# A gMLP layer and a sliding-window attention layer on one core: k's low part at full height over zeros, and both sets of PSUM banks for q, k with v, and z

## The chip, the core and the metric

The kernel runs on one core of one Trainium2 chip. The metric is the device time of one execution in microseconds (us); three runs of the kernel before gave a median of 1056.93 us (1056.63 to 1057.12). Profiles are taken of one execution, with a row for each instruction of each engine: PE (TensorE, matrix products; its weight loads are listed as PEld), DVE (VectorE), ACT (ScalarE), POOL (GpSimd) and SP (SyncE, which here only issues DMAs).

## The reference

1024 tokens of width 1024, float32. One gMLP layer, then one attention layer with 16 query heads over 4 shared key/value heads of width 64, a window of 128, attention sinks and ALiBi. Cut to what matters:

```python
u, v, z = split(rms_norm(h) @ w_in, 3)                 # gMLP, width 2048
v = layer_norm(gelu(v))
s = einsum('gts,bnsgc->bntgc', tril(w_s), v) + b_s     # inside chunks of 128 tokens
h = h + rms_norm((gelu(u) * s * silu(z)) @ w_out)
kv_in = rms_norm(h)
k, v = kv_in @ w_k, kv_in @ w_v                        # 4 heads of 64
q, z = split(rms_norm(h) @ b_w_in, 2)
logits = (q / 8) @ k.T + alibi                         # block of 128 queries, 256 keys
p = exp(logits - m); o = (p @ v) / (sum(p) + exp(sink - m))
h = h + rms_norm((o * silu(z)) @ b_w_out)
```

## The kernel before

Nearly every product is made from operands in the fp32r form, split into a high part and a low part (hi = rounded, lo = rest), as three products hi*hi, hi*lo and lo*hi that accumulate in one PSUM bank (`mm3`, lines 168 to 171). ACT makes the high part and DVE the low part, of weights (`split`, `split_scaled`, lines 104 to 110) as of activations. PSUM has two sets of four banks of 128 x 512: tag "mm" and tag "s" (`bank`, line 81).

The stages stand one behind another: the v layer (to about 150 us), u and z with the spatial mixing (to about 500 us), the first output layer, and from about 653 us the attention layer, in two halves of 512 tokens, h = 0 and h = 1. In its order, lines 1197 to 1226:

1. `q_phase(0)`: q of half 0 in two groups of four row blocks of 128 (`qz_four`), each group 4 weight pieces x 24 products into four "mm" banks (tiles qz). ACT and DVE move each bank out in two steps each (lines 969 and 970): q_hi holds the high part of q for the even head's 64 rows and the low part in the other 64 rows, q_lo the other way round. Beside it runs `chain_a(1)`, the residual sum of half 1, and the first steps of `norm_h1(1)`.
2. `kv_phase(0)`: k and v of half 0 (tiles pk, pv; lines 987 to 1013), in four "mm" banks. The high part of k goes into all 128 rows of kh[par] (the same 64 rows twice), its low part into 64 rows of one tile kl.
3. `z_phase(0)`: z of half 0, two groups in "mm" banks, and between its products the rest of `norm_h1(1)`: 8 groups of four transposes (tiles nt, line 769) into "s" banks, which ACT and DVE split into n1.
4. `attn(0)`: units of one block of 128 queries and one pair of key heads. `scores` (lines 1022 to 1065) makes, twice per unit, two banks of scores with 8 products: four of full height (128 rows: q's high and low part against the doubled kh, lines 1040 to 1044), then four of half height (64 rows: q's high part against kl, lines 1045 to 1050). The softmax follows on DVE and ACT, `transposes` (tiles pt) on PE, the causal masks on POOL (tiles pc, pp), `values` (tile o, products 64 columns wide), and the gate and the split on DVE and ACT. Between those steps `fill` hands out products of k, v, q and z of half 1.
5. `attn(1)`, with the last z and the output layer of half 0 (`out_b0`) as its fill; then `out_b1`.

Inside a program each engine runs its instructions in a fixed order. That order comes from a scheduler which may move independent instructions past each other, so it is not the text's. The weights go through two buffers of whi and wlo: piece n+2 can be split once the products of piece n are done.

In the v layer (`v_layer`, lines 291 to 505) the products come in steps (Q, m, u); after a step ACT moves banks out, and the lines 492 to 496 (`late`) apply the gelu to four tiles of a past sum and store them.

Of the kernel before, what the change touches and what calls it, by code (L numbers as in the profile page):

```python
# [50 lines left out]
def tile_yoco(  # L51
# [239 lines left out]
    def v_layer(ahead):  # L291
# [141 lines left out]
        for n, (Q, m, u) in enumerate(steps):  # L433
# [19 lines left out]
            if n == 0:  # L453
                xload(xa[:, 1], 0, 1, 0, 2)
            elif n == 1:
                prep(3)
                xload(xa[:, 1], 0, 1, 2, 2)
            elif n >= 4:
                step(side)
            if u == 0:  # L460
                continue
# [29 lines left out]

            late = {6: (a1, 0), 4: (e67, 1)}.get(m) if Q == 0 else None
            if late:
                for t in range(4):
                    done(late[0][t], late[0][t], late[1], late[1], t, Q)
                store(slots[late[1]], late[1], late[1], Q)
# [263 lines left out]
    def norm_h1(h, n, yo):  # L760
        for t in range(4):
# [180 lines left out]
    kl = bp.tile([P, 2, S], F32R, name="kl")  # L942
# [8 lines left out]
    def qz_four(h, which, m, n, evac):  # L951

        ps = [bank("mm", f"qz{h}_{which}_{m + i}") for i in range(4)]
# [33 lines left out]
    def kv_phase(h, n):  # L987
# [18 lines left out]
        hs = slice(h * TH, (h + 1) * TH)  # L1006
        for i in range(2):
            for par in range(2):
# [3 lines left out]
                nc.vector.tensor_tensor(kl[rw, i, hs], pk[i][rw], kh[par][rw, i, hs].bitcast(F32), ALU.subtract)  # L1012
            nc.vector.tensor_copy(vt[:, h * 4 + 2 * i:h * 4 + 2 * i + 2].rearrange("p a b -> p (a b)"), pv[i])

    class Unit:
# [6 lines left out]
        def scores(self, gp):  # L1022
# [16 lines left out]

            for g in range(2):  # L1040
                m = p * 4 + gp * 2 + g
                for par in range(2):
                    nc.tensor.matmul(pss[par][:, g, w0:256], lhsT=q[par][:, m, bs_], rhs=kh[par][:, p, ks],
                                     start=g == 0, stop=False, skip_group_check=True)
            for g in range(2):
                m = p * 4 + gp * 2 + g
                for par in range(2):
                    rw = half[par]
                    nc.tensor.matmul(pss[par][:, g, w0:256], lhsT=q[par][rw, m, bs_], rhs=kl[rw, p, ks],
                                     start=False, stop=g == 1, skip_group_check=True)  # L1050
# [80 lines left out]
    def out_b0(y, yo, gp):  # L1131
        ss = const.tile([P, 2, 4], F32, tag="ss", name="ssb0")
        for gd in range(2):
            ps = [bank("mm", f"ob0_{gd}_{t}") for t in range(4)]
            for cp in range(4):
                hi, lo = wnext()
                for j in range(2):
# [7 lines left out]
                    yield  # L1145
            for t in range(4):
                evac_out(yo[t], ss, ps[t], t, gd, gp, "ob0")
# [10 lines left out]
    def final(h, t, yo, ss, r=None):  # L1158
        r = final_rstd(h, t, ss) if r is None else r
        xt = load_tok(h1d[h][t], f"hf{h}_{t}")  # L1160
        for i in range(2):
            cs = slice(i * 512, i * 512 + 512)
            nc.vector.scalar_tensor_tensor(yo[:, cs], yo[:, cs], r, xt[:, cs], ALU.mult, ALU.add)
            if (h, t) == (1, 3) or i == 1:
                cs = cs if (h, t) == (1, 3) else slice(0, D)
                (nc.scalar if (h, t, i) == (1, 3, 1) else nc.sync).dma_start(
# [121 lines left out]
```

## Time and profile before

| | |
|---|---|
| median of 3 runs | 1056.93 us |
| the profiled execution, its own time | 1056.3 us |
| its span, first to last instruction | 1054.4 us |
| mean granted TensorE clock | 0.999 |
| busy: PE, DVE, ACT, POOL | 1042.8, 731.9, 577.0, 194.7 us |

Read it so: a row of the timeline has the start and the length of an instruction in us, its engine, its line, its output and inputs, their shapes, and how often it follows itself; behind it, in brackets, the idle time of the engine before it and whose end ended that. Products overlap in the array, so the length of one is not what it costs. What it costs is the distance from its start to the start of the next one: two of 128 x 512 start 0.227 us apart in undisturbed stretches.

### The profile page before, as it was taken

To read this page: it belongs to the slowest core of one execution; us is meant where nothing else is said; L and a number is where in the kernel's file an instruction comes from. 1 tells how busy PE (TensorE), PEld (TensorE's weight loads), DVE (VectorE), ACT (ScalarE), POOL (GpSimd) and SP (SyncE) were. 2 spreads that over 40 slices of the span, in tenths; PEclk is the share of its full clock that TensorE was granted. 3 is DMA by queue.
4 is the path that set the end of the run, shared out by engine and by line. 5 is a ranking of instruction groups with operands and counts; after the bars stand their busy time and mean duration, and the time that the engine had idled before them with its cause. 6 is when DMAs were issued, how large, how long until landed. Compare 5 with 4: busy or idle time off the path is not lost.

```text
span 1054.4 us, 13649 instructions
## 1 busy us (share of the span) xinstructions
PE 1042.8 (99%) x4994; PEld 849.3 (81%) x4994; DVE 731.9 (69%) x1244; ACT 577.0 (55%) x989; POOL 194.7 (18%) x151
## 2 busy tenths in 40 slices
PE   9999999999999999999999999999999999999997
PEld 7788788888888888888888888788887777777776
DVE  7987467867767768678696587745257876667763
ACT  6684443555565555555444474645466665686631
POOL 0500003254343542540200000000000111011120
PEclk9999999999999999999999999999999999999999
DMA  8877352334333434338997542632222121221363
GB/s 319 270 274 265 100 180 83 122 110 138 119 116 115 150 106 134 111 131 279 328 337 273 190 149 93 210 100 91 94 75 72 40 81 61 80 61 60 121 218 120
DMA packets 79890, 157.55 MB, mean 149 GB/s; under 512 B 5712, under 2 KB 32592, under 8 KB 79824
## 3 DMA queue, kind: packets, MB, share of 16 engines
q1 hardware_dynamic: 75168, 147.75, 41.2%
q10 hardware_dynamic: 4656, 8.94, 2.4%
q8 instruction: 39, 0.64, 0.2%
q14 instruction: 27, 0.22, 0.1%
HBM read 125.21 MB, written 31.46 MB: 149 GB/s over the span
## 4 chain that ended last, share of the span: by engine, by line
PE 92%; DVE 4%; issue 2%; DMA 1%; ACT 0%; POOL 0%; DVEq 0%; POOLq 0%; ACTq 0%
PE ob L169 6%; PE ub L169 6%; PE ub L171 6%; PE ob L170 6%; PE ub L170 6%; PE ob L171 6%; PE qz L169 5%; PE qz L170 5%; PE qz L171 5%; PE uc L170 3%; PE uc L169 3%; PE uc L171 3%; PE sp L614 3%; PE vb L169 2%; PE vb L170 2%; PE vb L171 2%
## 5 line engine op out<-in xcount | busy, mean ns | idle before, releaser
L169 PE MATMUL qz<-n_hi,whi 128*128 128x512 f32 x256 | 102.8, 402 | 2.2 <-DVE q_lo L970 2.1
L110 DVE SCALAR_TENSOR_TENSOR wlo<-raw_w,gn,whi 128x512 fp32r<-128x512 f32 x80 | 58.3, 758 | 63.9 <-ACT whi L109 63.6
L170 PE MATMUL qz<-n_lo,whi 128*128 128x512 f32 x256 | 100.0, 391 | 0.0
L171 PE MATMUL qz<-n_hi,wlo 128*128 128x512 f32 x256 | 99.9, 390 | 0.0
L109 ACT ACTIVATE whi<-raw_w,gn 128x512 fp32r<-128x512 f32 x80 | 54.6, 716 | 55.6 <-PE qz L170 25.8
L1064 ACT ACTIVATE pr<-pr,mx 128x129 f32<-128x129 f32 x128 | 50.0, 393 | 42.1 <-DVE mx L1060 41.8
L169 PEld LDWEIGHTS qz<-n_hi,whi 128*128 128x128 f32 x256 | 48.0, 188 | 21.3 <-issue 9.2
L105 ACT ACTIVATE uzhilo_g<-f 128x1024 fp32r<-128x1024 f32 x31 | 32.9, 1060 | 49.7 <-PE uc L171 43.8
L171 PEld LDWEIGHTS qz<-n_hi,wlo 128*128 128x128 f32 x256 | 48.1, 188 | 10.5
L170 PEld LDWEIGHTS qz<-n_lo,whi 128*128 128x128 f32 x256 | 48.1, 188 | 9.0
L106 DVE TENSOR_TENSOR uzhilo_g<-f,uzhilo_g 128x1024 fp32r<-128x1024 f32 x31 | 38.6, 1246 | 20.1 <-ACT uzhilo_g L105 20.1
L209 ACT ACTIVATE uz_slots<-ub 128x512 f32<-128x512 f32 x48 | 28.3, 589 | 42.1 <-PE ub L171 38.9
L169 PE MATMUL ub<-T,whi_g 128*128 128x512 f32 x128 | 50.7, 396 | 0.0
L169 PE MATMUL ub<-T,uzhilo_g 128*128 128x512 f32 x128 | 50.5, 395 | 0.0
L171 PE MATMUL ub<-T,wlo_g 128*128 128x512 f32 x128 | 49.9, 390 | 0.0
L171 PE MATMUL ub<-T,uzhilo_g 128*128 128x512 f32 x128 | 49.9, 390 | 0.0
L170 PE MATMUL ub<-T,uzhilo_g 128*128 128x512 f32 x128 | 49.8, 389 | 0.0
L170 PE MATMUL ub<-T,whi_g 128*128 128x512 f32 x128 | 49.8, 389 | 0.0
L169 PE MATMUL uc<-T,uzhilo_g 128*128 128x512 f32 x124 | 48.9, 395 | 0.0
L170 PE MATMUL uc<-T,uzhilo_g 128*128 128x512 f32 x124 | 48.3, 389 | 0.0
L171 PE MATMUL uc<-T,uzhilo_g 128*128 128x512 f32 x124 | 48.3, 389 | 0.0
L105 ACT ACTIVATE whi_g<-raw_uz 128x1024 fp32r<-128x1024 f32 (+1 forms) x31 | 26.5, 854 | 36.9 <-PE ua L170 14.6
(326 smaller groups left out, 3058.9 us busy)
## 6 DMA issues: line engine op xcount, KB each, us to landing
raw_uz<-in_wuz_in_dram SPq DMA_DIRECT2D x32, 512.0 KB, 3.4
raw_w<-in_wqz_dram SPq DMA_DIRECT2D x32, 512.0 KB, 3.5
td<-uz_slots SPq DMA_DIRECT2D x56, 256.0 KB, 2.1
orawP2a<-td SPq DMA_DIRECT2D x28, 512.0 KB, 4.0
raw<-in_wv_in_dram SPq DMA_DIRECT2D x17, 512.0 KB, 4.7
vg<-vd SPq DMA_DIRECT2D x8, 1024.0 KB, 5.3
orawP2b<-in_wo_a_dram SPq DMA_DIRECT2D x16, 512.0 KB, 8.0
vraw<-in_wv_in_dram SPq DMA_DIRECT2D x13, 512.0 KB, 4.8
```

The costliest lines, as they stand in the source:

```text
L105: nc.scalar.activation(hi, src, AF.Copy)
L106: nc.vector.tensor_tensor(lo, src, hi.bitcast(F32), ALU.subtract)
L109: nc.scalar.activation(hi, src, AF.Copy, scale=g)
L110: nc.vector.scalar_tensor_tensor(lo, src, g, hi.bitcast(F32), ALU.mult, ALU.subtract)
L169: nc.tensor.matmul(out, lhsT=a_hi, rhs=b_hi, start=start, stop=False, skip_group_check=True)
L170: nc.tensor.matmul(out, lhsT=a_hi, rhs=b_lo, start=False, stop=False, skip_group_check=True)
L171: nc.tensor.matmul(out, lhsT=a_lo, rhs=b_hi, start=False, stop=stop, skip_group_check=True)
L209: nc.scalar.activation(out, a, AF.Copy)
L614: nc.tensor.matmul(psv[:, n], lhsT=d["vg"][:, 4 * j + n, i * P:(i + 1) * P], rhs=d["wc"], start=True, stop=True)
L1064: nc.scalar.activation(pr[:, i], pr[:, i], AF.Exp, bias=mx[:, i:i + 1], scale=-1.0, accum_out=dn[:, i:i + 1])
```

## The change

Four edits that belong together, and two that follow from them.

- The low part of k gets two tiles, kl[0] and kl[1], each 128 rows high, with k's low part in the head's own 64 rows and zeros in the other 64, which POOL writes once (`memset`). The low product of a score now reads all 128 rows of q[par]. The loop puts the low product of a bank right behind its high product.
- kl[1] lies in the buffer P1_3, which held two token blocks of `yo` of half 1. So `norm_h1(1)` takes the blocks in the order 2, 3, 0, 1, and runs between the products of `kv_phase(0)`, not of `z_phase(0)`.
- The second group of q and the first group of z of half 0 go into "s" banks.
- P1_3 is taken until the end of attention, so the output of half 0 is kept in two halves: columns 0 to 511 in P1_0, columns 512 to 1023 in the weight buffers whi and wlo. Each token block of the final output is stored with two DMAs of 512 columns, not one of 1024.
- In the v layer the four late gelus with their store stand one step (24 products) later.

```diff
--- before.py
+++ after.py
@@ -457,6 +457,12 @@
                 xload(xa[:, 1], 0, 1, 2, 2)
             elif n >= 4:
                 step(side)
+
+            late = {(7, 0): (a1, 0), (3, 0): (e67, 1)}.get((m, u)) if Q == 0 else None
+            if late:
+                for t in range(4):
+                    done(late[0][t], late[0][t], late[1], late[1], t, Q)
+                store(slots[late[1]], late[1], late[1], Q)
             if u == 0:
                 continue
             for t in range(4):
@@ -488,12 +494,6 @@
                 block = (slots[0], 0, 0) if m == 2 else (slots[1], 1, 1)
             if block:
                 store(*block, Q)
-
-            late = {6: (a1, 0), 4: (e67, 1)}.get(m) if Q == 0 else None
-            if late:
-                for t in range(4):
-                    done(late[0][t], late[0][t], late[1], late[1], t, Q)
-                store(slots[late[1]], late[1], late[1], Q)
             if m == 3:
                 a1, e67 = [], []
             if Q == 1 and m == 2:
@@ -757,8 +757,8 @@
         rstd(r1[h], s1, f"h1{h}")
         yield
 
-    def norm_h1(h, n, yo):
-        for t in range(4):
+    def norm_h1(h, n, yo, order=range(4)):
+        for t in order:
             xt = st.tile([P, D], F32, tag="xt", name=f"hb{h}_{t}")
             nc.vector.tensor_scalar(xt, yo[t], r1[h][:, t:t + 1], None, ALU.mult)
             yield
@@ -939,7 +939,8 @@
     nc.vector.memset(neg, -1e30)
 
     kh = [bp.tile([P, 2, S], F32R, name=f"kh{i}") for i in range(2)]
-    kl = bp.tile([P, 2, S], F32R, name="kl")
+
+    kl = [bp.tile([P, 2, S], F32R, name="kl0")]
     qsc = bp.tile([P, 2], F32, name="qsc")
     nc.sync.dma_start(out=qsc, in_=consts[:, C_QS:C_QS + 2])
     snk = bp.tile([P, 4, 4], F32, name="snk")
@@ -950,7 +951,8 @@
 
     def qz_four(h, which, m, n, evac):
 
-        ps = [bank("mm", f"qz{h}_{which}_{m + i}") for i in range(4)]
+        tag = "s" if (h, which, m) in ((0, 0, 4), (0, 1, 0)) else "mm"
+        ps = [bank(tag, f"qz{h}_{which}_{m + i}") for i in range(4)]
         for kq in range(4):
             hi, lo = (t.rearrange("p (m k c) -> p m k c", m=4, k=2) for t in wnext())
             for i in range(4):
@@ -1004,12 +1006,17 @@
                         hi[:, vs], lo[:, vs], k == 0 and t4 % 2 == 0, k == KT - 1 and t4 % 2 == 1)
                 yield
         hs = slice(h * TH, (h + 1) * TH)
+        if h == 0:
+            kl.append(big.tile([P, 2, S], F32R, tag="P1_3", name="kl1"))
+            for par in range(2):
+                zero = kl[par][half[1 - par]].bitcast(F32)
+                nc.gpsimd.memset(zero.rearrange("p a b -> p (a b)"), 0.0)
         for i in range(2):
             for par in range(2):
                 rw, ot = half[par], half[1 - par]
                 nc.scalar.activation(kh[par][rw, i, hs], pk[i][rw], AF.Copy)
                 nc.scalar.activation(kh[par][ot, i, hs], pk[i][rw], AF.Copy)
-                nc.vector.tensor_tensor(kl[rw, i, hs], pk[i][rw], kh[par][rw, i, hs].bitcast(F32), ALU.subtract)
+                nc.vector.tensor_tensor(kl[par][rw, i, hs], pk[i][rw], kh[par][rw, i, hs].bitcast(F32), ALU.subtract)
             nc.vector.tensor_copy(vt[:, h * 4 + 2 * i:h * 4 + 2 * i + 2].rearrange("p a b -> p (a b)"), pv[i])
 
     class Unit:
@@ -1036,18 +1043,12 @@
                 pss.append(bank("s", f"s{self.id}_{gp}{par}").rearrange("p (g s) -> p g s", g=2))
             ks = slice(b * P - P + w0, (b + 1) * P)
 
-
             for g in range(2):
                 m = p * 4 + gp * 2 + g
                 for par in range(2):
-                    nc.tensor.matmul(pss[par][:, g, w0:256], lhsT=q[par][:, m, bs_], rhs=kh[par][:, p, ks],
-                                     start=g == 0, stop=False, skip_group_check=True)
-            for g in range(2):
-                m = p * 4 + gp * 2 + g
-                for par in range(2):
-                    rw = half[par]
-                    nc.tensor.matmul(pss[par][:, g, w0:256], lhsT=q[par][rw, m, bs_], rhs=kl[rw, p, ks],
-                                     start=False, stop=g == 1, skip_group_check=True)
+                    for k, w in enumerate((kh, kl)):
+                        nc.tensor.matmul(pss[par][:, g, w0:256], lhsT=q[par][:, m, bs_], rhs=w[par][:, p, ks],
+                                         start=g + k == 0, stop=g + k == 2, skip_group_check=True)
             for par in range(2):
                 ps = pss[par]
                 c = ps[:, :, P:256]
@@ -1143,8 +1144,16 @@
                         if t == 1:
                             yield
                     yield
+            if gd == 0:
+                t0 = big.tile([P, 4, 512], F32, tag="P1_0", name="yb0")
+                yo.append([t0[:, t] for t in range(4)])
+            else:
+
+                t1 = [wpool.tile([P, 2, 512], F32, tag=tag, name=f"yb0{tag}") for tag in ("whi", "wlo")]
+                yo.append([t1[t // 2][:, t % 2] for t in range(4)])
             for t in range(4):
-                evac_out(yo[t], ss, ps[t], t, gd, gp, "ob0")
+                sumsq(ss[:, gd, t:t + 1], ps[t], f"ob0_{gd}_{t}")
+                nc.vector.tensor_tensor(yo[gd][t], ps[t], gp[:, gd * 512:gd * 512 + 512], ALU.mult)
         return ss
 
     def final_rstd(h, t, ss):
@@ -1160,11 +1169,9 @@
         xt = load_tok(h1d[h][t], f"hf{h}_{t}")
         for i in range(2):
             cs = slice(i * 512, i * 512 + 512)
-            nc.vector.scalar_tensor_tensor(yo[:, cs], yo[:, cs], r, xt[:, cs], ALU.mult, ALU.add)
-            if (h, t) == (1, 3) or i == 1:
-                cs = cs if (h, t) == (1, 3) else slice(0, D)
-                (nc.scalar if (h, t, i) == (1, 3, 1) else nc.sync).dma_start(
-                    out=out[h * TH + t * P:h * TH + (t + 1) * P, cs], in_=yo[:, cs])
+            nc.vector.scalar_tensor_tensor(yo[i], yo[i], r, xt[:, cs], ALU.mult, ALU.add)
+            (nc.scalar if (h, t, i) == (1, 3, 1) else nc.sync).dma_start(
+                out=out[h * TH + t * P:h * TH + (t + 1) * P, cs], in_=yo[i])
 
     def out_b1(y, yo, gp, ss0, yo0):
         ss = const.tile([P, 2, 4], F32, tag="ss", name="ssb1")
@@ -1189,9 +1196,9 @@
                 else:
                     evac_out(yo[t], ss, ps, t, gd, gp, "ob1")
                 if gd == 0:
-                    final(0, t, yo0[t], ss0)
+                    final(0, t, [yo0[i][t] for i in range(2)], ss0)
                 else:
-                    final(1, t, yo[t], ss, r)
+                    final(1, t, [yo[t][:, 0:512], yo[t][:, 512:1024]], ss, r)
                 yield
 
     side = chain_a(1, yo, ss)
@@ -1203,21 +1210,20 @@
     drain(side)
     gp = post_gain(b_post, "gpb")
     n1 = pair("P2", "n1")
-    side = norm_h1(1, n1, yo)
-    step(side)
-    drain(kv_phase(0, n0))
+    side = norm_h1(1, n1, yo, (2, 3, 0, 1))
     z0, z1 = ([big.tile([P, 4, TH], F32, tag=f"P1_{2 * i}", name=f"z{h}_{i}") for i in range(2)]
               for h in range(NH))
-    for _ in z_phase(0, n0, z0, 0, 8):
+    for _ in kv_phase(0, n0):
         step(side)
     drain(side)
+    drain(z_phase(0, n0, z0, 0, 8))
     q1 = pair("P3", "q1")
     fill = chain(kv_phase(1, n1), q_phase(1, n1, q1), z_phase(1, n1, z1, 0, 4))
     attn(0, q0, z0, fill, 64)
     drain(fill)
 
     def tail():
-        yo = yo_alloc((3, 0), "yb0")
+        yo = []
         ss = yield from out_b0(q0, yo, gp)
         yield from out_b1(q1, yo_alloc((1, 2), "yb1"), gp, ss, yo)
```

What it does to the order on the engines, at three places. First PE, one block of scores with the products behind it (half 0, unit of block 1 and pair 1; s_1_10 and s_1_11 are the two banks). Before:

```order
L1043 MATMUL s_1_10_6574<-kh_4948,q_hi 128x256
L1043 MATMUL s_1_11_6575<-kh_4949,q_lo 128x256
L1043 MATMUL s_1_10_6574<-kh_4948,q_hi 128x256
L1043 MATMUL s_1_11_6575<-kh_4949,q_lo 128x256
L1049 MATMUL s_1_10_6574<-kl,q_hi 128x256
L1049 MATMUL s_1_11_6575<-kl,q_lo 128x256
L1049 MATMUL s_1_10_6574<-kl,q_hi 128x256
L1049 MATMUL s_1_11_6575<-kl,q_lo 128x256
L169 MATMUL qz_0_4_6524<-n_hi,whi_6528 128x512
```

And now:

```order
L1050 MATMUL s_1_10_6577<-kh_4948,q_hi 128x256
L1050 MATMUL s_1_10_6577<-kl_4950,q_hi 128x256
L1050 MATMUL s_1_11_6578<-kh_4949,q_lo 128x256
L1050 MATMUL s_1_11_6578<-kl_5544,q_lo 128x256
L1050 MATMUL s_1_10_6577<-kh_4948,q_hi 128x256
L1050 MATMUL s_1_10_6577<-kl_4950,q_hi 128x256
L1050 MATMUL s_1_11_6578<-kh_4949,q_lo 128x256
L1050 MATMUL s_1_11_6578<-kl_5544,q_lo 128x256
L169 MATMUL qz_0_4_6527<-n_hi,whi_6531 128x512
```

The high and low product of a bank now follow each other with the same weights, all 128 rows high. In one unit (block 3, pair 0) the order of before puts twelve other products between the first six and the last two of a block; now they stand between the first five and the last three.

Second PE in the second group of q of half 0 (qz0_0_4 to qz0_0_7 are its four banks, whi4 and whi5 its first two weight pieces). Before:

```order
L171 MATMUL qz0_0_5_5145<-n0_hi_4571,wlo4_5097 128x512
L169 MATMUL qz0_0_4_5144<-n0_hi_4571,whi5_5148 128x512
L169 MATMUL qz0_0_6_5146<-n0_hi_4571,whi4_5096 128x512
L170 MATMUL qz0_0_6_5146<-n0_lo_4572,whi4_5096 128x512
L171 MATMUL qz0_0_6_5146<-n0_hi_4571,wlo4_5097 128x512
L169 MATMUL qz0_0_6_5146<-n0_hi_4571,whi4_5096 128x512
```

And now:

```order
L170 MATMUL qz0_0_7_5147<-n0_lo_4572,whi4_5096 128x512
L171 MATMUL qz0_0_7_5147<-n0_hi_4571,wlo4_5097 128x512
L169 MATMUL qz0_0_4_5144<-n0_hi_4571,whi5_5148 128x512
L170 MATMUL qz0_0_4_5144<-n0_lo_4572,whi5_5148 128x512
L171 MATMUL qz0_0_4_5144<-n0_hi_4571,wlo5_5149 128x512
L169 MATMUL qz0_0_4_5144<-n0_hi_4571,whi5_5148 128x512
```

Before, the first product of piece 5 stood ahead of bank 6; now it stands behind bank 7, where the text has it.

Third DVE, from the end of q of half 0 into k and v (wlo9 to wlo12 are low parts of weight pieces, 8 to 11 being those of k and v; n1_lo is the low part of the transposed blocks, hb the scaled ones). Before:

```order
L110 SCALAR_TENSOR_TENSOR wlo9_5303<-raw_w9_5218,gn_80,whi9_5302 128x512
L970 SCALAR_TENSOR_TENSOR q0_lo_4958<-qz0_0_7_5147,qsc_4951,q0_lo_4958 64x512
L110 SCALAR_TENSOR_TENSOR wlo10_5347<-raw_w10_5250,gn_80,whi10_5346 128x512 x2
L110 SCALAR_TENSOR_TENSOR wlo11_5391<-raw_w11_5308,gn_80,whi11_5390 128x512 x2
L110 SCALAR_TENSOR_TENSOR wlo12_5435<-raw_w12_5352,gn_80,whi12_5434 128x4x128 x2
L1012 TENSOR_TENSOR kl_4950<-pk0_0_5298,kh0_4948 64x512
```

And now:

```order
L110 SCALAR_TENSOR_TENSOR wlo9_5305<-raw_w9_5218,gn_80,whi9_5304 128x512
L972 SCALAR_TENSOR_TENSOR q0_lo_4958<-qz0_0_7_5147,qsc_4951,q0_lo_4958 64x512
L106 TENSOR_TENSOR n1_lo_5295<-nt1_2_0_5332,n1_hi_5294 128x4x128
L106 TENSOR_TENSOR n1_lo_5295<-nt1_2_1_5339,n1_hi_5294 128x4x128
L763 TENSOR_SCALAR hb1_0_5394<-yoa1_2_4272,r1_1_90 128x1024
L110 SCALAR_TENSOR_TENSOR wlo10_5381<-raw_w10_5250,gn_80,whi10_5380 128x512
L106 TENSOR_TENSOR n1_lo_5295<-nt1_3_0_5366,n1_hi_5294 128x4x128
L106 TENSOR_TENSOR n1_lo_5295<-nt1_3_1_5373,n1_hi_5294 128x4x128
L110 SCALAR_TENSOR_TENSOR wlo10_5381<-raw_w10_5250,gn_80,whi10_5380 128x512
L763 TENSOR_SCALAR hb1_1_5428<-yoa1_2_4272,r1_1_90 128x1024
L106 TENSOR_TENSOR n1_lo_5295<-nt1_0_0_5408,n1_hi_5294 128x4x128
```

The splits of pieces 10 and 11 were next to each other; now their halves stand behind low parts that wait for transposes on PE. The split of piece 9 is done ahead of all of them.

## The prediction

> **What bounds the kernel now.** I read the profile's page first, then the list of waits on PE, then the timeline of PE at the places that the change touches, because the page leaves little else to ask.
>
> ```profile
> span 1054.4 us, 13649 instructions
> PE 1042.8 (99%) x4994; PEld 849.3 (81%) x4994; DVE 731.9 (69%) x1244; ACT 577.0 (55%) x989; POOL 194.7 (18%) x151
> ```
>
> PE is busy for 99% of the span, and in the chain that ended last it has the first share:
>
> ```profile
> PE 92%; DVE 4%; issue 2%; DMA 1%; ACT 0%; POOL 0%; DVEq 0%; POOLq 0%; ACTq 0%
> ```
>
> So a microsecond counts if PE gives it back: a wait of PE that goes, or products that start closer to each other. An engine beside it counts only where PE waits for it. The waits on PE, the two longest:
>
> ```profile
> PE qz L169 <- DVE q_lo L970: 2.1, 2, 1.7
> PE vb L169 <- ACT ve L209: 1.2, 1, 1.2
> ```
>
> The first is the one that the change aims at: a product of the second group of q waits for a bank of the first. The second, in the v layer, stays as it is: the copy waited for there stands behind the first of the late gelus in ACT's order, before and now; only the three gelus behind it move. The late gelus I therefore cost at nothing: their work on ACT and DVE is the same, one step of 24 products (5.4 us) later, and no other PE wait of that layer is in the list. If that cover fails, a copy that comes late costs PE at most what the row above shows, 1.2 us.
>
> **The scores.** Here is one block on PE's timeline, after transposes and ahead of ordinary products:
>
> ```profile
> 844.34 0.36 PE L1043 MATMUL s<-kh,q_hi 128*128 128x256 f32 x1
> 844.54 0.28 PE L1043 MATMUL s<-kh,q_lo 128*128 128x256 f32 x1
> ...
> 844.98 0.39 PE L1049 MATMUL s<-kl,q_lo 64*128 64x256 f32 x1
> 845.21 0.28 PE L1049 MATMUL s<-kl,q_hi 64*128 64x256 f32 x1
> 845.21 0.28 PE L1049 MATMUL s<-kl,q_lo 64*128 64x256 f32 x1
> 845.42 0.50 PE L169 MATMUL qz<-n_hi,whi 128*128 128x512 f32 x1
> 845.76 0.40 PE L170 MATMUL qz<-n_lo,whi 128*128 128x512 f32 x1
> ```
>
> And the other kind, ahead of the value products (o), which are 64 columns wide:
>
> ```profile
> 862.02 0.28 PE L1043 MATMUL s<-kh,q_hi 128*128 128x256 f32 x1
> ...
> 862.37 0.28 PE L1043 MATMUL s<-kh,q_lo 128*128 128x256 f32 x1
> 862.58 0.39 PE L1049 MATMUL s<-kl,q_hi 64*128 64x256 f32 x1
> ...
> 863.02 0.66 PE L1096 MATMUL o<-pc,vt 128*64 128x512 f32 x2
> ```
>
> Look at the starts. Four full-height products start 0.117 us apart (862.02 to 862.37 are three such steps). From the last of them to the first half-height one it is 0.21, so changing the height costs 0.09. The half-height ones start two at a time, 0.23 from pair to pair: 0.115 for each, as much as a full-height one. So half height saves nothing per product here, and it costs a change on the way in (0.09), one on the way out (0.21 to the next start, 0.09 over 0.117), and 0.11 more on the first ordinary product behind it (845.42 to 845.76 is 0.34, where undisturbed ones are 0.23 apart).
>
> Now the block at full height. First kind: 0.20 to the second product as now (that step belongs to the transposes ahead), seven steps of 0.117, and 0.23 to the second ordinary product: 0.20 + 0.82 + 0.23 = 1.25, where 844.34 to 845.76 is 1.42. Gain 0.17. Second kind: 1.00 now. The change to the narrow value products stays, and costs as much from full height:
>
> ```profile
> 876.37 0.39 PE L171 MATMUL qz<-n_hi,wlo 128*128 128x512 f32 x1
> 876.68 1.09 PE L1096 MATMUL o<-pc,vt 128*64 128x512 f32 x4
> ```
>
> 0.31 instead of 0.23, so 0.09. At full height: eight steps of 0.117 and 0.09 make 1.03, a loss of 0.03.
>
> There are 32 blocks: 8 units in each half, 2 blocks in each. The value products follow the first block of a unit from the third unit on, 6 in a half, 12 in all; 20 blocks are of the first kind. 20 x 0.17 - 12 x 0.03 = 3.0. One block is cut in two by other products in the order of before, and pays the way out and in once more: 0.3. Four of the blocks are only half as wide (128 keys); I count them like the others. Sum of the scores: 3.3 us. From below, the 0.11 on the first product behind might belong to something else: 20 x 0.06 + 0.3 - 0.4 = 1.1. From above, that the first kind also saves what the next few products lose to 0.24 and 0.23, some 0.03 each: 3.9. I take 3.3, since these are the rows of the very place.
>
> **The second group of q.** With "s" banks, free since the transposes of half 0, the wait goes. What is late next?
>
> ```profile
> 675.79 0.39 PE L171 MATMUL qz<-n_hi,wlo 128*128 128x512 f32 x1
> 677.91 0.47 PE L169 MATMUL qz<-n_hi,whi 128*128 128x512 f32 x1 [1.73 <-DVE q_lo L970]
> 678.22 0.39 PE L170 MATMUL qz<-n_lo,whi 128*128 128x512 f32 x1
> 684.06 0.39 PE L170 MATMUL qz<-n_lo,whi 128*128 128x512 f32 x1
> ```
>
> ```profile
> 682.50 0.75 DVE L110 SCALAR_TENSOR_TENSOR wlo<-raw_w,gn,whi 128x512 fp32r<-128x512 f32 x1
> ```
>
> The group could start at 676.02. Up to 684.06 PE makes 25 products (24 of the first weight piece and one of the next): 25 x 0.227 = 5.67, so 8.04 - 5.67 = 2.37 us are lost, the wait and the slower starts behind it. DVE moves the first group out without a pause and has the two halves of the next piece's low part in that queue, in the same order now as before; the second half is done at 683.25. PE, starting at 676.02, needs it for its 30th product, at 676.02 + 29 x 0.227 = 682.60. So a wait of 0.65 stays, and the slow start behind a wait (677.91 to 678.22, 0.08 over) with it. Gain 2.37 - 0.73 = 1.6. Bounds: 2.4 if DVE gets there sooner, 0.6 if its queue slips by another 1 us (POOL zeroes kl[1] at that time, next part).
>
> **k and v, and z.** The same bank wait in small stands at the start of k and v:
>
> ```profile
> 701.08 0.40 PE L170 MATMUL pk<-n_lo,whi 128*128 128x512 f32 x1
> 701.59 0.47 PE L169 MATMUL pk<-n_hi,whi 128*128 128x512 f32 x1
> 701.90 0.40 PE L170 MATMUL pk<-n_lo,whi 128*128 128x512 f32 x1
> ```
>
> 0.51 - 0.23 and 0.31 - 0.23, together 0.36, are lost; with the change these banks will have been empty for a group's length. At z, four transposes with the wait in front of the product behind them, and four without:
>
> ```profile
> 723.27 0.60 PE L769 MATMUL nt<-ident,hb 128*128 128x128 f32 x4
> 724.00 0.47 PE L169 MATMUL qz<-n_hi,whi 128*128 128x512 f32 x1
> ...
> 725.46 0.60 PE L769 MATMUL nt<-ident,hb 128*128 128x128 f32 x4
> 725.81 0.48 PE L169 MATMUL qz<-n_hi,whi 128*128 128x512 f32 x1
> ```
>
> The four with the wait take 0.73, the others 0.35, so 0.38; and the transposes now stand in four groups where they stood in five, one change less, 0.09. Together 0.36 + 0.47 = 0.8. Bounds 0.1 and 1.0.
>
> The transposes moved into k and v queue their splits on DVE ahead of the low parts of pieces 10 and 11. A half step of k and v is 6 products of 0.227 and 12 of 0.117, 2.8 us. Piece 11's second half is split behind the last pair of transposes, which stands after the fourth half step; with at most four DVE steps of 0.75 and the same on ACT it is there 6 us later, and it is needed three half steps (8.4 us) later. Cost nothing; the cover is 2.4 us.
>
> **The rest.** The zeroes of kl are two new instructions on POOL, 64 x 2048 each; no row shows their length.
>
> ```profile
> 658.84 1.01 POOL L179 TENSOR_TENSOR rpa<-rpa,small 128x4 f32<-128x4 f32 x1 [37.84 <-DVE rpa L178]
> ```
>
> ```profile
> L206 POOL TENSOR_TENSOR uz_slots<-uz_slots 128x512 f32<-128x512 f32 x17 | 28.2, 1657 | 0.5
> ```
>
> By the slowest POOL row per element they take 4 x 1.66 = 6.6 us. The first stands ahead of the row at 658.84, in 37.84 us of idle time; the second follows at about 676 and is needed by the first scores after 770. Both are covered. The output of half 0 in other buffers has the same steps; its seven more DMAs are SP's, which no engine waits for, and the last block's stores are the same. Nothing.
>
> Sum: 3.3 + 1.6 + 0.8 = 5.7 us. The profiled execution took 1056.3, so 1050.6; the median of 1056.93 is 0.6 above it, so 1051.2.
>
> **The rivals.** First, the waits return elsewhere: with 2.4 us less of waiting, PE meets weight pieces or banks that are late, and the parts on q, k, v and z give nothing. For it speaks that piece 5 shows just this with 0.65 us; against it, that DVE is idle again soon after. Only the scores gain: 1056.93 - 3.3 = 1053.6. Chance 0.14.
>
> Second, another engine becomes the bound of the attention:
>
> ```profile
> 858.91 1.09 POOL L1082 TENSOR_SCALAR_AFFINE_SELECT pc<-pc 128x1024 f32<-128x1024 f32 x1
> ...
> 931.55 1.09 POOL L1082 TENSOR_SCALAR_AFFINE_SELECT pc<-pc 128x1024 f32<-128x1024 f32 x1
> ```
>
> ```profile
> 932.82 1.08 PE L1096 MATMUL o<-pc,vt 128*64 128x512 f32 x4
> ```
>
> The value products at 932.82 start 0.18 after their mask is done at 932.64, and PE will be there 0.14 sooner: just enough. At 863.02 the cover is 3.02 (860.00). If it were everywhere as at 932.82, or worse, the scores' gain would be waited away: 1056.93 - 2.4 = 1054.5. Chance 0.07.
>
> Third, on the other side: the pair of half-height products runs side by side, so that its 0.23 is the time of one of them, and at full height each low product pays it alone. Then a block of the first kind takes 0.20 + 3 x 0.117 + 4 x 0.23 + 0.23 = 1.70, 0.28 more than now, and one of the second 4 x 0.117 + 4 x 0.23 + 0.09 = 1.48, 0.48 more: 20 x 0.28 + 12 x 0.48 = 11.4 lost against 2.4 gained, 1065.9. It decides as soon as a low product at full height takes over 0.15. For it speaks that the two of a pair start together; against it the full-height products of the same width beside them, which take 0.117. Chance 0.05. The Trainium skill, "TensorE: Matmul & The Clock Gate", section "Part 3: Packing small matmuls", says that products in different row groups of the array run concurrently, and so speaks against giving that up. The trace agrees that they start together, and not that it saves: 0.23 for a pair is no less than two full ones.
>
> **How the numbers follow.** The forecast has the remaining 0.74. Its own range: scores 1.1 to 3.9, q 0.6 to 2.4, the rest 0.1 to 1.0, hardly all at one end: 3.0 to 7.0 less, 1049.9 to 1053.9. A measurement of this kernel can tell about 0.2%, 2.1 us, from no change. Faster by more than that (below 1054.8) are the forecast, most of the first rival and half of the second: 0.88. Within it: their tails, 0.07. Slower: 0.05. The range 1049.3 to 1054.3 holds the forecast and the first rival.
>
> **What would show it.** The rows of 64*128 are gone and score products start 0.117 apart throughout; behind them the next product starts after 0.12, with no 0.34 after that. Of the waits of qz for q_lo, 2.1 in two, only the shorter is left, 0.4 (2.1 - 1.7), and a wait of 0.65 for wlo stands in the other's place. In k and v no waits of PE. Wrong would make it: low products 0.2 apart; a wait of PE for wlo or n_lo between 700 and 725; more than 0.5 us of waits of o for pc.

## The result, and the profile after

The changed kernel takes 1051.38 us, the median of six runs (1050.98 to 1051.72); the kernel before, run beside it, 1057.01 us (1056.32 to 1058.06). The ratio is 0.9945, with a 95% interval of 0.9934 to 0.9957: 5.6 us less, where the sum of the prediction was 5.7. The profiled execution took 1051.56 us, 4.7 us less than the one of before.

The head of its page and the chain that ended last:

```profile
span 1049.8 us, 13661 instructions
PE 1039.2 (99%) x4994; PEld 854.8 (81%) x4994; DVE 731.9 (70%) x1244; ACT 577.2 (55%) x989; POOL 195.2 (19%) x153
```

```profile
PE 93%; DVE 4%; ACT 1%; issue 0%; DMA 0%; POOL 0%; DVEq 0%; POOLq 0%; ACTq 0%
```

PE has as many instructions as before and is as full. The time went out of its starts and waits. Cut at the first product of q, of k and v, of the scores, and at the last value product, PE's timeline gives these stages (us; the tail is taken to the start of PE's last product):

| | q | k, v, z | attention | tail |
|---|---|---|---|---|
| before | 45.90 | 70.66 | 238.35 | 38.55 |
| after | 45.36 | 69.52 | 235.16 | 38.55 |
| less | 0.54 | 1.14 | 3.19 | 0 |
| forecast | 1.6 | 0.8 | 3.3 | 0 |

Behind that last product the program has grown. On PE's timeline before, then after:

```profile
1047.72 0.39 PE L171 MATMUL ob<-wob_hi,q_lo 128*128 128x512 f32 x1
```

```profile
1042.68 0.39 PE L171 MATMUL ob<-wob_hi,q_lo 128*128 128x512 f32 x1
```

From these starts to the end of the span (1054.4 and 1049.8) it is 6.7 us before and 7.1 after. All three profiles that keep the old stores have 6.7, all eleven with the new ones 7.1 to 7.2, so 0.4 to 0.5 us go here. The last store lands equally late in all of them, 5.7 us behind the start of PE's last product; the growth comes behind that landing, and why was not tried.

**The scores.** A block of the first kind on PE's timeline, then one of the second:

```profile
841.44 0.37 PE L1050 MATMUL s<-kh,q_hi 128*128 128x256 f32 x1
841.65 0.28 PE L1050 MATMUL s<-kl,q_hi 128*128 128x256 f32 x1
...
842.48 0.40 PE L169 MATMUL qz<-n_hi,whi 128*128 128x512 f32 x1
842.71 0.40 PE L170 MATMUL qz<-n_lo,whi 128*128 128x512 f32 x1
...
858.82 0.28 PE L1050 MATMUL s<-kh,q_hi 128*128 128x256 f32 x1
...
859.85 0.66 PE L1097 MATMUL o<-pc,vt 128*64 128x512 f32 x2
```

From the first score product to the second ordinary one it is 1.27 (841.44 to 842.71), forecast 1.25; to the first value product 1.03 (858.82 to 859.85), as forecast.

**q.** The wait for a bank is gone, and two waits for the low part of piece 5 stand in its place:

```profile
682.57 0.50 PE L171 MATMUL qz<-n_hi,wlo 128*128 128x512 f32 x1 [0.66 <-DVE wlo L110]
...
683.14 0.40 PE L170 MATMUL qz<-n_lo,whi 128*128 128x512 f32 x1
684.12 0.51 PE L171 MATMUL qz<-n_hi,wlo 128*128 128x512 f32 x1 [0.59 <-DVE wlo L110]
```

The prediction had one such wait, 0.65 for the second half; here both halves are late, 1.25. DVE's queue slipped. This is where, on DVE's timeline after and then before:

```profile
668.22 1.28 DVE L753 SCALAR_TENSOR_TENSOR yoa<-yoa,rpa,xa 128x1024 f32<-128x1024 f32 x1 [1.09 <-DMA xa<-in_x_dram]
```

```profile
667.37 1.28 DVE L753 SCALAR_TENSOR_TENSOR yoa<-yoa,rpa,xa 128x1024 f32<-128x1024 f32 x1
```

The load of x for half 1 was issued 0.16 earlier than before (662.64 for 662.80), as PE's program too is 0.16 earlier at that place, and it took about 1 us longer to land. DVE waited for it, and all that stands behind it on DVE came later. The experiments tell whether that is the change's doing.

**The list of waits.** From 654 to 770 us, the stages of q, k, v and z, PE waits for nothing else:

```profile
PE qz L171 <- DVE wlo L110: 1.2, 2, 0.7
```

From 760 us on the one wait of before, 0.4, is left as forecast, and no wait of a value product for its mask is listed:

```profile
PE qz L169 <- DVE q_lo L972: 0.4, 1, 0.4
```

### The profile page after: what moved, and what is told of

It is laid out like the page before. It is cut to its first block, busy times and chain, and to the rows that moved or that the text cites. A ratio compares the mean times of both kernels' runs of the same rounds, so it can differ in the third digit from the quotient of the medians.

```text
span 1049.8 us, 13661 instructions
## 1 busy us (share of the span) xinstructions
PE 1039.2 (99%) x4994; PEld 854.8 (81%) x4994; DVE 731.9 (70%) x1244; ACT 577.2 (55%) x989; POOL 195.2 (19%) x153
## 4 chain that ended last, share of the span: by engine, by line
PE 93%; DVE 4%; ACT 1%; issue 0%; DMA 0%; POOL 0%; DVEq 0%; POOLq 0%; ACTq 0%
PE ob L169 6%; PE ub L169 6%; PE ub L171 6%; PE ob L171 6%; PE ob L170 6%; PE ub L170 6%; PE qz L169 5%; PE qz L171 5%; PE qz L170 5%; PE uc L169 3%; PE uc L171 3%; PE uc L170 3%; PE s L1050 3%; PE sp L614 3%; PE vb L170 2%; PE vb L171 2%
## 5 line engine op out<-in xcount | busy, mean ns | idle before, releaser
L105 ACT ACTIVATE uzhilo_g<-f 128x1024 fp32r<-128x1024 f32 x31 | 32.9, 1060 | 48.6 <-PE uc L171 42.7
```

Source lines behind the costliest of these rows:

```text
L105: nc.scalar.activation(hi, src, AF.Copy)
```

## The experiments

Times are medians; each kernel has its own interval against the kernel before, run beside it. Where less than that counts, PE's stages in the trace decide.

### The half height alone, put back

```diff
-                    for k, w in enumerate((kh, kl)):
-                        matmul(.., lhsT=q[par][:, m, bs_], rhs=w[par][:, p, ks])
+                    matmul(.., lhsT=q[par][:, m, bs_], rhs=kh[par][:, p, ks])
+            for g in range(2):
+                for par in range(2):
+                    rw = half[par]
+                    matmul(.., lhsT=q[par][rw, m, bs_], rhs=kl[par][rw, p, ks])
```

> The changed kernel with one thing undone: the low score products are 64 rows high again, four behind the four high ones; tiles, banks, places of the transposes stay as changed. My theory (the height is what the scores pay for, 3.3 us as forecast, and it adds to the rest): 1054.7 us (1054.0 to 1055.4), blocks ahead of ordinary products 1.42 us again, PE's waits in q, k, v and z as in the changed kernel. Rival (what the scores gained came from elsewhere, from the banks or from where the transposes stand): under 1052.5 us.

Measured: 1054.05 us (1053.73 to 1054.42), ratio 0.9969 [0.9957, 0.9981]. The attention takes 237.84 us in the trace, 2.68 more than after; k, v and z take 69.52, as after. So the height is worth 2.7 us, and it adds to the rest. The block that other products cut in two is cut in this kernel as well, and has 0.33 of the 2.7. 0.5 us of the attention's 3.19 stay gained with the half height, most of it in steps of 0.03 to 0.04 between the blocks; what makes these I did not try.

### The order of the full-height products

The four high products first, then the four low ones, all 128 rows high:

```diff
             for g in range(2):
                 for par in range(2):
-                    for k, w in enumerate((kh, kl)):
-                        matmul(.., lhsT=q[par][:, m, bs_], rhs=w[par][:, p, ks])
+                    matmul(.., lhsT=q[par][:, m, bs_], rhs=kh[par][:, p, ks])
+            for g in range(2):
+                for par in range(2):
+                    matmul(.., lhsT=q[par][:, m, bs_], rhs=kl[par][:, p, ks])
```

> The changed kernel, with all eight score products 128 rows high, but in the order of before: four high ones, then four low ones. My theory (only the height counts): no difference to the changed kernel, 1051.4 us (1050.8 to 1052.0), starts 0.117 us apart. Rival (a high and a low product behind each other use the same weights, and that is where something is saved): 20 to 30 blocks lose 0.05 us or more each, 1052.5 us or more.

Measured: 1051.62 us (1051.06 to 1052.07), ratio 0.9944 [0.9932, 0.9957]; the attention takes as long as after (3.19 less than before). The order, and the same weights twice in a row, are worth nothing.

### What a half-height product costs: three runs

First, the half-height kernel with the two low products of one head behind each other:

```diff
-            for g in range(2):
-                for par in range(2):
+            for par in range(2):
+                for g in range(2):
```

> The half-height kernel again, but the four low products in another order: the two of the even head (rows 0 to 63) behind each other, then the two of the odd head (rows 64 to 127), so that no two that follow each other lie in different rows, but for one place. Theory A (a half-height product takes 0.115 us by itself, the pair that starts together is only how the records look): as the half-height kernel, 1054.7 us, within 1. Theory B (my third rival's picture: two in different rows run side by side, and each takes 0.23 us): the four low products take some 0.7 to 0.9 us for 0.46, 0.25 to 0.46 more in each of 32 blocks, 8 to 15 us more: 1063 to 1070 us.

Measured: 1055.01 us (1054.33 to 1055.50), ratio 0.9976 [0.9967, 0.9985]; within 1 us of the half-height kernel, so theory A by the letter. But its timeline warns against it:

```profile
843.07 0.39 PE L1055 MATMUL s<-kl,q_hi 64*128 64x256 f32 x1
843.07 0.38 PE L1055 MATMUL s<-kl,q_lo 64*128 64x256 f32 x1
843.29 0.28 PE L1055 MATMUL s<-kl,q_hi 64*128 64x256 f32 x1
843.29 0.28 PE L1055 MATMUL s<-kl,q_lo 64*128 64x256 f32 x1
```

The text of the kernel has the two of q_hi first and the two of q_lo behind them, and still one of each starts at 843.07 and one of each at 843.29. Whether the scheduler put them back into pairs, or PE started them so whatever their order, this view does not show. Either way the run couldn't tell the theories apart. Leaving one head out can:

```diff
-                for par in range(2):
+                for par in range(1):
```

> The half-height kernel without the low products of the odd heads, so that two half-height products follow each other where two pairs did (this leaves a part of the scores out). If half-height products run one after another at 0.115 us: 0.23 less in each block, 7 us under the half-height kernel, 1047 us. If the two of a pair run side by side: no difference, 1054 us within 0.7.

Measured: 1055.66 us (1054.95 to 1056.49), ratio 0.9984 [0.9975, 0.9994]. A block, with half of its low products left out:

```profile
843.76 0.36 PE L1049 MATMUL s<-kh,q_hi 128*128 128x256 f32 x1
...
844.19 0.28 PE L1049 MATMUL s<-kh,q_lo 128*128 128x256 f32 x1
844.40 0.51 PE L1055 MATMUL s<-kl,q_hi 64*128 64x256 f32 x2
844.83 0.50 PE L169 MATMUL qz<-n_hi,whi 128*128 128x512 f32 x1
845.17 0.39 PE L170 MATMUL qz<-n_lo,whi 128*128 128x512 f32 x1
```

843.76 to 845.17 is 1.41, as with all of them (1.42 before). The low products of the other head cost nothing beside these: the pair does run side by side. The kernel is 1.6 us longer, not shorter, for reasons outside of these blocks, which I did not follow; the scheduler puts its products in another order, with the value products in 17 stretches for 16.

Then what is the 0.23 from pair to pair? The low products twice, so that four pairs follow each other:

```diff
-            for g in range(2):
+            for r in range(4):
+                g = r % 2
```

> The half-height kernel with its four low products made twice, so that eight half-height products stand in a row (the low part is added twice: this changes the result). It asks what a pair costs inside a run of pairs. If each half-height product takes 0.115 us, as I read it in the prediction, or a pair takes 0.23: four more of them are 0.46 in a block, 14 us over the half-height kernel, 1068 us. If the pair runs side by side in 0.117, and the rest of the 0.23 of the first pair belongs to the change of height (a change then costs 0.09 on the step itself and 0.11 on the product behind it, 0.2 in all, as the kernel with seven changes shows: 0.31 from start to start): two more pairs are 0.23 in a block, 7 us over, 1061 us.

Measured: 1060.55 us (1059.58 to 1061.36), ratio 1.0032 [1.0021, 1.0044]: 6.5 us over the half-height kernel. The block, with one row for each of the four pairs:

```profile
843.96 0.28 PE L1049 MATMUL s<-kh,q_lo 128*128 128x256 f32 x1
844.17 0.39 PE L1056 MATMUL s<-kl,q_hi 64*128 64x256 f32 x1
...
844.40 0.28 PE L1056 MATMUL s<-kl,q_lo 64*128 64x256 f32 x1
844.52 0.28 PE L1056 MATMUL s<-kl,q_hi 64*128 64x256 f32 x1
...
844.64 0.28 PE L1056 MATMUL s<-kl,q_lo 64*128 64x256 f32 x1
844.84 0.50 PE L169 MATMUL qz<-n_hi,whi 128*128 128x512 f32 x1
845.18 0.40 PE L170 MATMUL qz<-n_lo,whi 128*128 128x512 f32 x1
```

Only the first pair takes 0.23. The second and the third start 0.12 after the one ahead: a pair of half-height products costs as much as one full-height product, half of what two full-height ones cost. What eats that up is the change of height. It costs 0.09 on the step itself (843.96 to 844.17 is 0.21 for 0.12, 844.64 to 844.84 the same) and 0.11 on the step behind it (0.23 for 0.12, 0.34 for 0.23), so 0.2 on the way in and 0.2 on the way out. The Trainium skill, "TensorE: Matmul & The Clock Gate", section "Part 3: Packing small matmuls", says that products in different row groups run concurrently; these rows agree, with 0.12 for a pair. The Trainium skill, "TensorEngine Tiling (Array Packing)", section "Key Properties", says without a number that a change of the tiling mode drains the engine. These rows show a price of 0.2 us for each change, and not what it is made of.

### Height changed at every product

```diff
+                    for k, w in enumerate((kh, kl)):
+                        rw = half[par] if k else slice(0, P)
+                        matmul(.., lhsT=q[par][rw, m, bs_], rhs=w[par][rw, p, ks])
```

> The half-height products again, each low one right behind its high one, so that the height changes seven times in a block where the half-height kernel changes once. If each change costs 0.09 us as read from the trace of before, and a low product 0.115: 6 x 0.09 x 32 = 17 us over the half-height kernel, about 1072 us. If a low product alone takes 0.23, another 4 x 0.115 x 32 = 15 us: about 1087 us. If a change costs nothing by itself: about 1055 us.

Measured: 1097.11 us, one run; the attention is 42.7 us longer than before. A block:

```profile
870.46 0.36 PE L1051 MATMUL s<-kh,q_hi 128*128 128x256 f32 x1
870.75 0.38 PE L1051 MATMUL s<-kl,q_hi 64*128 64x256 f32 x1
871.06 0.38 PE L1051 MATMUL s<-kh,q_lo 128*128 128x256 f32 x1
```

From the second product on each start is 0.31 after the one ahead, 0.12 and one change of 0.2. All three numbers expected were too low, since each priced a change at 0.09 or at nothing. Against the half-height kernel there are six more changes of 0.2 in a block, and two pairs that no longer run side by side at 0.117 each, so 1.43. The blocks that are 256 keys wide and stand together got 1.39 to 1.41 longer, the narrow ones 1.1; all blocks together make the 43.2 us by which the attention is longer than in the half-height kernel.

### One set of banks

```diff
-        tag = "s" if (h, which, m) in ((0, 0, 4), (0, 1, 0)) else "mm"
+        tag = "mm"
```

> The changed kernel with the second group of q and the first of z back in the first set of banks; full-height scores and the places of the transposes stay. My theory (the bank waits come back, at q 2.4 us lost against 1.8 with two sets, at k and v 0.4 to 0.6, at z 0.3 to 0.4): 1.2 to 2.0 us over the changed kernel, 1052.6 to 1053.4 us. Rival (the moved transposes cover those waits by themselves): within 0.6 us of the changed kernel, up to 1052.0 us.

Measured: 1055.84 us (1054.17 to 1056.72), ratio 0.9984 [0.9975, 0.9992], 4.5 us over the changed kernel in the medians and 3.0 in the profiled executions: more than either theory had. The bank wait of q is back, on PE's list:

```profile
PE qz L169 <- DVE q_lo L972: 2.4, 2, 2.0
```

q takes 46.15 us; k, v and z take 71.63, of which some 0.4 are three score products that the scheduler now puts ahead of z. That leaves 71.2, 0.6 more than in the kernel before. There the transposes at the start of z stand in front of the wait for k and v's banks; moved into k and v, with one set of banks, they cover nothing. The two edits need each other, and as an undo of one this run is not clean.

### q's second group alone

The kernel before, with this edit only:

```diff
-        ps = [bank("mm", f"qz{h}_{which}_{m + i}") for i in range(4)]
+        tag = "s" if (h, which, m) == (0, 0, 4) else "mm"
+        ps = [bank(tag, f"qz{h}_{which}_{m + i}") for i in range(4)]
```

> The kernel before with one thing changed: the second group of q of half 0 goes into the second set of banks. My theory: the bank wait of 1.73 us goes, waits for the low part of weight piece 5 take its place; if the loads of x land as in the profile of before, 0.65 to 0.75 of them are left (gain 1.6), if they land 1 us later, as in the profile of the changed kernel, 1.25 (gain 0.5): 1055.3 to 1056.4 us. Rival (the whole bank wait is gained): 1054.6 us.

Measured: 1054.57 us (1053.64 to 1056.25, leaving aside one run of 3272), ratio 0.9975 [0.9964, 0.9986]: 2.3 us less, more than expected, and as the rival had it by the time alone. The trace puts it elsewhere: q takes 44.63, 1.27 less, with one wait of 0.6 for wlo; the other 0.62 come from k and v, whose banks are now free in time. My sum for this run had left those out. The rest of the time is the start of the program, 0.8 us shorter by chance.

### The kernel before, profiled again

> The kernel before, for another profile of it. Its times so far lie in two groups, about 1056.5 and about 1058.1 us; the times of the changed kernel lie in one. My theory: in the second group the loads of x for half 1 land about a microsecond later, DVE's moves of q's first group out of its banks come that much later, and PE's wait of 1.73 us for the bank grows to 2.5 to 3.5 us, while the two sets of banks take that wait off; so a run of about 1056.5 shows a load of x in time and a wait of about 1.7 us, a run of about 1058.1 a DVE wait for xa and a longer wait. Rival: the difference lies in another stage.

Measured: 1057.24 us, between the two groups. DVE, then PE:

```profile
668.31 1.28 DVE L753 SCALAR_TENSOR_TENSOR yoa<-yoa,rpa,xa 128x1024 f32<-128x1024 f32 x1 [0.83 <-DMA xa<-in_x_dram]
```

```profile
675.99 0.39 PE L171 MATMUL qz<-n_hi,wlo 128*128 128x512 f32 x1
678.83 0.47 PE L169 MATMUL qz<-n_hi,whi 128*128 128x512 f32 x1 [2.46 <-DVE q_lo L970]
```

The same kernel, with the load 0.75 us later, waits 2.46 for the bank, not 1.73. So the late load is chance, and not the change's. And q's length follows it one for one in all profiles in which PE still waits there. With DVE's wait for xa ahead of this row:

| kernel | wait for xa | q | q less the wait |
|---|---|---|---|
| before | 0.08 | 45.90 | 45.82 |
| before, again | 0.83 | 46.62 | 45.79 |
| one set | 0.33 | 46.15 | 45.82 |
| low products twice | 0.26 | 44.48 | 44.22 |
| late gelus as before | 0.49 | 44.67 | 44.18 |
| half height | 0.66 | 44.94 | 44.28 |
| after | 1.09 | 45.36 | 44.27 |

Five more profiles in which q has both sets of banks and PE waits for wlo have 44.3 in the last column. Like against like the change takes 45.81 - 44.24 = 1.57 off q. The 0.54 of the two profiles is this less 1.01 of a later load. No run of about 1058 was profiled, so what makes up the rest of that group stays open.

### The late gelus

```diff
-            late = {(7, 0): (a1, 0), (3, 0): (e67, 1)}.get((m, u)) if Q == 0 else None
...
+            late = {6: (a1, 0), 4: (e67, 1)}.get(m) if Q == 0 else None
```

> The changed kernel with the four late gelus of the v layer and their store where they stood before. My theory (they are worth nothing; the wait of vb in the v layer ends at a fixed time, so it takes up what the start of the program came later): 1051.4 us (1050.9 to 1051.9), and the start of the first product of vb at about 53.5 us in the trace as in both kernels. Rival (the shorter wait there in the changed kernel, 0.34 for 1.19 us, is their doing): 0.8 us more, 1052.2 us.

Measured: 1051.32 us (1050.94 to 1051.91), ratio 0.9942 [0.9928, 0.9955]; no difference to the changed kernel. The wait of vb is 1.18 us in this trace, 0.34 in the changed kernel's, 1.2 in eight others that have the gelus where the changed kernel has them, and 0.5 in a ninth. It varies from run to run, and its end does too (53.87 here, 53.54 before, 53.38 after), so that a fixed end, as I expected, is not what the trace shows.

### Piece 5 split first

The changed kernel, with the split of piece 5 ahead of three of the four moves out of q's first banks:

```diff
-                if kq == 3:
+                if kq == 3 and (h, which, m) == (0, 0, 0):
+                    if i == 3:
+                        weights.split(weights.at + 1)
+                    for j in {0: (0,), 3: (1, 2, 3)}.get(i, ()):
+                        evac(m + j, ps[j])
+                elif kq == 3:
                     evac(m + i, ps[i])
```

> The changed kernel, and in addition the split of weight piece 5 stands ahead of three of the four moves of q's first group out of its banks, which nothing waits for now. My theory (the two waits for that piece's low part are all that is left at q, 1.25 us and 0.5 for the slower starts behind them): PE runs through q with no wait over 0.2 us, 1.0 to 1.8 us under the changed kernel, 1049.6 to 1050.4 us. Rival (the next thing is late at once: piece 6, or k and v's banks): within 0.5 us of the changed kernel.

Measured: 1050.08 us (1049.21 to 1050.63), ratio 0.9929 [0.9917, 0.9942]; 1.3 us under the changed kernel. q takes 43.52 with the load 0.85 late, and PE has no wait from 654 to 725 us. That also shows that nothing else was due there. In the next experiment's profile, which has this split too, the load is 0.46 late and q takes 43.52 again: q no longer follows the load.

### Half height only ahead of value products

The kernel with piece 5 split first, with `scores(0)` of the units from the third on as in the first experiment:

```diff
-                units[i].scores(0)
+                units[i].scores(0, int(i >= 2))
```

> The kernel with piece 5 split first, and in it the 12 score blocks that stand ahead of value products with their low products in half-height pairs, four high ones first; the other 20 blocks stay at full height. By the price of a change of height as the runs have it (0.09 on the step and 0.11 on the product behind it), these blocks pay 0.2 on the way in, the way out is paid to the value products anyway, and two pairs in 0.117 each save 0.23: 0.03 less in each of 11 blocks that are 256 keys wide (1.00 us from the first score product to the first value product, for 1.03), 0.3 us in the trace of the attention, 1049.8 us. If the half-height products cost 0.115 each, as the prediction had it, the trace shows the same here, so this run can't tell these two apart; it asks if the rule gives a kernel that is faster than both. Rival (the blocks' order or the softmax behind it pays it back): no less in the attention than in the kernel with piece 5 split first.

Measured: 1050.22 us (1049.66 to 1050.69), ratio 0.9930 [0.9918, 0.9943], the same as without. The blocks that stand together take 0.996 us for 1.030, as expected. One of the twelve does not stand together, and pays for it:

```profile
801.17 0.38 PE L1061 MATMUL s<-kl,q_hi 64*128 64x256 f32 x1
801.48 0.50 PE L169 MATMUL qz<-n_hi,whi 128*128 128x512 f32 x1
...
804.43 0.38 PE L1061 MATMUL s<-kl,q_lo 64*128 64x256 f32 x1
```

The scheduler puts twelve ordinary products between its first low product and the others. That is one way out and one way in more, 0.4, and eats what the other eleven gain; the attention takes 235.22 us for 235.16. The rival was right on the time.

## Why the prediction was right, point by point

- **PE's starts and waits decide.** Right: the stages add up to 1.57 (at like loads), 1.14 and 3.19, so 5.9, less the 0.4 to 0.5 behind PE's last product, which the forecast didn't have: about 5.4, against 5.6 with an interval of 4.5 to 7.0. The forecast of 5.7 comes closer than its terms do, since the part of k, v and z, which was too low, and the longer end, which was left out, cancel in part; that is luck.
- **The scores, 3.3.** The attention gave 3.19, but the height alone is worth 2.7, as the half-height kernel shows; the other 0.5 were not forecast, so that the agreement is in part luck. Block by block the sum held where the blocks are 256 keys wide: 0.15 to 0.17 less in the first kind, 0.03 more in the second, 0.35 less in the block that is cut in two. Counting the four narrow blocks like the others was too much: three gave 0.07 each, and the one ahead of value products lost 0.08. The reason behind the sum was wrong. The step "0.115 for each, as much as a full-height one. So half height saves nothing per product here" failed: the pair runs side by side and takes 0.12 in a run of pairs. The 0.23 between the only two pairs of a block is 0.12 and the 0.11 that belongs to the way in. Two pairs save 0.23, and the two changes cost 0.4: 0.17 left over, the same sum from other terms. Ahead of value products only the way in counts, 0.2 against 0.23: the 0.03.
- **The third rival** had the pair side by side right, and wrong that 0.23 is the time of one. The prediction's own sentence there, that the trace does not show the pair save anything, holds for two pairs only: with four pairs in a row the second and third take 0.12.
- **q, 1.6.** Right, 1.57, when the load of x lands at the same time. In the profile after it landed 1 us later, and the lower bound of that part (its queue slips by 1 us: 0.6) is what came out, 0.54. The same slip costs the kernel before as much.
- **k, v and z, 0.8.** Too low, 1.14. A row was missed in the trace of before: the first product of v (pv) starts late as well, which the prediction didn't count. On PE's timeline of before:

```profile
702.83 0.39 PE L170 MATMUL pk<-n_lo,whi 128*128 128x512 f32 x1
703.16 0.36 PE L169 MATMUL pv<-whi,n_hi 128*128 128x256 f32 x1
703.36 0.28 PE L170 MATMUL pv<-wlo,n_hi 128*128 128x256 f32 x1
```

The steps are 0.33 and 0.20 for 0.23 and 0.12, 0.18 in all. With it the sum is 1.0; the last 0.1 stays open.

- **Costed at nothing.** Right for the late gelus (their own run) and for the zeroes. For the output of half 0 it is right on PE, whose tail takes 38.55 us in both, and not behind PE: of what the change touches only the stores come that late, and the program's end is 0.4 to 0.5 us longer with them. The zeroes take 2.21 and 1.80 us on POOL, not 6.6 each; the first start at 639.89, and there are 16.57 us from their end to POOL's next step:

```profile
639.89 2.21 POOL L1013 MEMSET kl<- 64x2048 f32 x1 [19.07 <-DVE ohiloP0b L106]
658.67 1.01 POOL L179 TENSOR_TENSOR rpa<-rpa,small 128x4 f32<-128x4 f32 x1 [16.57 <-DVE rpa L178]
```

- **The rivals on waits.** Waits that return elsewhere did so in one place, piece 5, as forecast. Masks bound the attention in one place at most, and by little: the tightest value product starts 0.06 behind its mask (928.59, the mask being done at 928.53) and 0.25 behind the score product ahead of it, where the others take 0.21. That is 0.04 us.

## What to carry to other kernels

Price a change of shape between neighbouring products by the steps on both sides of it, and take the price of a product from inside a run of its kind; the first and the last of a run carry the change. A free set of banks removes a wait only up to the next thing that is late, so move that one forward in the same edit: here the split of the next weight piece, 1.3 us. When two profiles are compared, look for loads that landed differently, and take their difference off first.

## What the runs showed of the hardware

In these rows the weights are not loaded ahead at a change of height. The weight loads (PEld) of the two ordinary products behind a block, in the half-height kernel and then in the changed one:

```profile
843.39 0.19 PEld L169 LDWEIGHTS qz<-n_hi,whi 128*128 128x128 f32 x1
843.49 0.19 PEld L170 LDWEIGHTS qz<-n_lo,whi 128*128 128x128 f32 x1
```

```profile
842.36 0.19 PEld L169 LDWEIGHTS qz<-n_hi,whi 128*128 128x128 f32 x1
842.48 0.19 PEld L170 LDWEIGHTS qz<-n_lo,whi 128*128 128x128 f32 x1
```

In the changed kernel the load for the first ordinary product starts at 842.36, 0.12 ahead of it (842.48), beside the last score product. In the half-height kernel it starts at 843.39, 0.21 behind the last pair (843.18), and its product is listed with the same start. The 0.2 us of a change fit that, since the row of loads starts anew; that it is the cause was not tried by itself.
